# A second buffer for one output tile, and Q, residual and two additions in other places of a hand-written order

## The chip, the cores and the metric

The kernel runs on one core of one Trainium2 chip. The time is the device time of one execution in microseconds (us); the median of several runs is given. TensorE (PE) multiplies matrices, VectorE (DVE), ScalarE (ACT) and GpSimd (POOL) work on tiles, and SyncE (SP) issues the transfers. Each engine works through its own queue in order and waits on semaphores for the others.

## The reference

One layer of an encoder: 4096 tokens, width 1024, an attention group of 8 heads (2 key/value heads, band of 128 tokens on each side) and a pooling group, each gated, then an output projection, a norm and the residual.

```python
h = rmsnorm(x, pre_norm_g[l])
proj = jnp.einsum('bsd,de->bse', h, w_in[l])
q, k, v, g_a, u_p, g_p = jnp.split(proj, splits, axis=-1)
...
a = banded_attention(q, k, v, rel_bias, attn_sink[l]) * jax.nn.silu(g_a)
p = multiscale_pool(u_p, pool_w[l], pool_scale[l]) * jax.nn.silu(g_p)
mixed = jnp.einsum('bse,ed->bsd', jnp.concatenate([a, p], axis=-1), w_out[l])
x = x + rmsnorm(mixed, post_norm_g[l])
```

Inside `banded_attention`, each block of 128 queries sees three blocks of keys: scores, plus a position bias, then a softmax with a sink logit, then the weighted sum of V.

## The kernel before

A float32 value is carried as two float16 numbers, a high part and the low part that it leaves; a product of two such pairs is three float16 matmuls. The first half of the program (to about 500 us) computes the pooling group and the gates. The second half, which the change edits, runs backwards over 16 units of 256 tokens (two query blocks each; `u` is the unit, `b` the block, `half` a group of four heads). It is one list, `plan`: every step is entered with a due time by `due(t, step, ...)`, the list is sorted by that time, and the sorted order is the order on every engine. So a due time is not a time that a step waits for; it only says which steps stand ahead of it in each queue. The main loop runs from block 31 down to block 2; for the last units the due times are written out one by one (`at_`).

One visit of a block and half: TensorE makes `scores` (L1272); VectorE adds the bias and takes the maximum (`logits`, L1295); ScalarE makes the exponentials (L1306); VectorE the denominators (L1313) and their reciprocals (L1316); ScalarE the float16 probabilities `pn` (L1328, `probs`); VectorE what these leave (L1336, `rests`); SP turns both by a DMA transpose into `pt` (L1345), which TensorE multiplies with V in `values` (L1422). `gate` (L1446) multiplies the result with the gate into `at`.

Q for the next unit comes in two halves: TensorE's `proj_q` (L1227) fills a PSUM bank, then `keep_q` calls `split`: ScalarE writes the high part (L1216) and VectorE the low part (L1217), and after that the bank is free for the next half.

The output projection of a unit is a Strassen-like scheme of seven products (`product`, L1572, twelve matmuls of 512 columns each). The pieces are summed in two tiles of 128x1024 float32, `mo0` and `mo1`, one for each block of the unit. `begin` opens the unit's tiles (`open_unit`) and copies the first product from bank 0 into the second half of `mo0` (L1590), after which the product `12` adds into that bank. `add` (L1611), `gain11` (L1600), `square` (L1595) and `gain` (L1606) finish the tiles; `mean` makes the norm's factor; `residual` (L1633) multiplies `mo` with the factor and adds the input `xr`; `store` (L1639) writes the result. The casts to float16 pairs for the products are L1474 on ScalarE and L1478 on POOL.

`residual` of a unit's `mo0` is due late, in the next unit's visit, so it stands in VectorE's queue beside that unit's softmax. `mo0` and `mo1` have one buffer each (`bufs=1`).

Of the kernel before, what the change touches and what calls it, by code (L numbers as in the profile page):

```python
# [8 lines left out]
F32 = mybir.dt.float32  # L9
# [8 lines left out]
P = 128  # L18
S = 4096
D = 1024  # L20
# [114 lines left out]
def hybrid_layer(ctx: ExitStack, tc, io, out):  # L135
# [74 lines left out]
    with ExitStack() as actx:  # L210
# [689 lines left out]
        for j in range(4):  # L900
            ld(9.5 + 0.1 * j, wut[:, j], io["w_uT"][j], 0.5, w=[f"wut{j}"])
            z = turn("sq")
            for half in range(2):
                t = U0 + 4 * j + 2 * half
# [284 lines left out]
    pb = ctx.enter_context(tc.tile_pool(name="pb", bufs=2, reuse_waits="tile"))  # L1189
# [53 lines left out]
    def due(t, fn, *args):  # L1243
        plan.append((t, len(plan), fn, args))
# [216 lines left out]
    def spare32(tile, i):  # L1461

        return spare16(tile, 2 * D * i, 2 * D).bitcast(F32)
# [64 lines left out]
    LO, HI = slice(0, 512), slice(512, D)  # L1528
# [50 lines left out]
    def open_unit(u):  # L1579
        if u > 1:  # L1580
            mo_t[u] = [
                pb.tile([P, D], F32, name=f"mo{u}_{i}", tag=f"mo{i}", bufs=1) for i in range(2)
            ]
        else:
            mo_t[u] = [spare32("x", 2 * u + i) for i in range(2)]
        ss_t[u] = pb.tile([P, 4], F32, name=f"ss{u}", tag="ss")

    def begin(u):
        open_unit(u)
        nc.scalar.copy(mo_t[u][0][:, HI], z_t[u, 0])  # L1590
# [61 lines left out]
    def pe(us, fn, *args):  # L1652

        due(now[0], fn, *args)
        now[0] += us
        return now[0]
# [14 lines left out]
        due(t + late + 0.5, keep_v, u)  # L1671

    def do_q(u, half, late=0.0, bank=1):
        due(pe(5.3, proj_q, u, half, bank) - half + late, keep_q, u, half)

    def attend(b, bank):
        t = pe(2.0, values, b, bank)
# [36 lines left out]
    def mix_p3(u):  # L1714
        t = pe(M, product, u, "s4", O22, 1, True)
        due(t, add, u, (0, HI), (0, HI), 1)
        due(t + 0.7, square, u, 0, 1)
        due(t + 1.4, gain, u, 0, HI)
        due(t + 4.0, mean, u, 0)
        due(t + 12.4, residual, u, 0, LO)  # L1720
        due(t + 13.1, residual, u, 0, HI)
        due(t + 13.8, store, u, 0, slice(0, D))

    def finish(u, i, t):

# [6 lines left out]
    u = NU - 1  # L1732
# [6 lines left out]

    due(now[0] + 1.0, lambda: nc.scalar.activation(dummy, mhalf, AF.Exp))  # L1740
    do_q(u, 0)
    now[0] += 1.0
    for b in reversed(range(2, NB)):
        u = b // 2
# [5 lines left out]
        visit(b, 0)  # L1750
        if b == NB - 1:
            do_q(u, 1, 2.8, 0)
            due(now[0] + 0.1, load_x, u - 2)
            now[0] += 2.5
# [14 lines left out]
        elif b % 2:  # L1769
            mix_p3(u + 2)  # L1770
            do_kv(u - 1)
            attend(b + 1, 0)
            visit(b, 1)
            mix_p4(u + 1)
            mix_p1(u + 1)
            mix_p6(u + 1)
            mix_p2(u + 1)
        else:
            do_q(u - 1, 0, 2.0 * (b == NB - 2))
            if b < NB - 2:  # L1780
                attend(b + 1, 0)
            visit(b, 1)
            do_q(u - 1, 1, 2.0 * (b == NB - 2), int(b < NB - 2))
            due(now[0] + 2.1, load_x, u - 3)
            if b == NB - 2:
                attend(b + 1, 1)
            elif b > 2:
                mix_p7(u + 1)
                mix_p5(u + 1)
# [15 lines left out]
    def at_(t, fn, *args):  # L1805
        due(z + t, fn, *args)
# [11 lines left out]
    def cast(th, tw, u, name, f, eng):  # L1818
        at_(th, high, u, name, f)
        at_(tw, low, u, name, f, eng)  # L1820
# [36 lines left out]
    soft(0, 0, 24.9, 25.6, 29.4, 29.5, 29.7, 31.7)  # L1857
    soft(0, 1, 31.6, 32.3, 36.5, 36.7, 36.8, 38.8)

    at_(4.8, add, 2, (1, HI), (0, HI), 0)  # L1860
    at_(5.5, add, 2, (1, LO), (1, HI), 2)
    at_(6.2, add, 2, (1, HI), (1, HI), 1)
    at_(7.0, square, 2, 1, 0)
# [19 lines left out]
    at_(19.1, gain11, 1)  # L1883
    at_(17.8, square, 1, 0, 0, 0)
    cast(23.5, 24.2, 1, "s1", a_s1, V)
    at_(23.45, add, 1, (0, HI), (0, HI), 1)
    cast(24.8, 25.0, 1, "s4", a12, G)
    at_(27.0, add, 1, (1, HI), (0, HI), 0)
    at_(27.7, add, 1, (1, LO), (1, HI), 2)
# [15 lines left out]
    at_(45.9, gate, 0)  # L1905
    cast(46.7, 47.3, 0, "21", a21, V)
    at_(30.0, open_unit, 0)
    for i, t in ((0, 48.5), (1, 53.7)):
        for c in range(2):
# [92 lines left out]
```

## Time and profile before

| | us |
|---|---|
| median of 3 runs | 1193.59 (1192.48 to 1194.16) |
| the profiled execution | 1192.04 |
| its span in the profile | 1190.3 |
| TensorE busy | 1154.4 (97%) |
| VectorE busy | 941.9 (79%) |
| ScalarE busy | 703.8 (59%) |
| POOL busy | 303.4 (25%) |

A row of the timeline gives the start, the duration, the engine, the line, the operation, the tile written and the tiles read, the shapes, how many equal instructions are drawn together, and in brackets how long the engine had been idle and what ended that. "SPq" is SyncE's queue. Matmuls overlap each other, and their ends are modelled.

### The profile page before, as it was taken

The page shows a single profiled execution, that of the slowest core. Times are in us where ns is not written, and L with a number is a line of the kernel's source. Part 1 is how long each engine was busy: PE and PEld are TensorE (multiplying, and loading weights), DVE is VectorE, ACT ScalarE, POOL GpSimd, SP SyncE. Part 2 cuts the span into 40 slices and gives each one's busy share as a digit, 9 for nine tenths or more (in the row PEclk, how much of TensorE's full clock was granted, in tenths as well). Part 3 has the DMA queues.
Part 4 walks back from the last instruction along what each step waited for, and adds up shares of the span by engine and source line. Part 5 has one row for each costly group of instructions (what it writes and reads, how often), then busy time and mean ns, then how long its engine had stood idle before and what let it go on. Part 6 is the DMA issues. An engine that isn't in the chain of part 4 may idle for free. (4 is left out here: it accounts for less than half of the span.)

```text
span 1190.3 us, 33985 instructions
## 1 busy us (share of the span) xinstructions
PE 1154.4 (97%) x14304; PEld 884.8 (74%) x14304; DVE 941.9 (79%) x1879; ACT 703.8 (59%) x1459; POOL 303.4 (25%) x309
## 2 busy tenths in 40 slices
PE   5999999999999999998999999999999999999997
PEld 4998888888988888876667667576666667757643
DVE  6889996867888973567877878877887787787796
ACT  5865555545755541265666576666667667666662
POOL 0002111101101110203334434433533443343231
PEclk9999999999999999999999999999999999999999
DMA  9544587577657573397966876787886678586694
GB/s 318 208 124 151 169 277 246 171 239 259 221 169 249 156 212 117 117 242 174 253 181 147 188 189 128 200 196 142 192 193 177 145 191 192 135 190 164 156 245 124
DMA packets 292441, 224.65 MB, mean 189 GB/s; under 512 B 210704, under 2 KB 251920, under 8 KB 287680
## 3 DMA queue, kind: packets, MB, share of 16 engines
q1 hardware_dynamic: 292288, 222.48, 69.7%
q8 instruction: 112, 1.84, 0.6%
q14 instruction: 41, 0.34, 0.1%
HBM read 113.37 MB, written 60.33 MB: 146 GB/s over the span
## 5 line engine op out<-in xcount | busy, mean ns | idle before, releaser
L634 PEld LDWEIGHTS <-wq 128*128 128x128 f16 x4104 | 401.3, 98 | 53.1 <-issue 2.8
L634 PE MATMUL y<-xt,wq 128*128 128x256 f16 x1512 | 204.1, 273 | 0.9 <-ACT cc L742 0.9
L1336 DVE SCALAR_TENSOR_TENSOR pn<-p,rd,pn 128x384 f16<-128x384 f32 (+1 forms) x256 | 155.6, 654 | 31.8 <-ACT pn L1328 31.8
L1227 PE MATMUL aq<-xb,xb 128*128 128x256 f16 x1024 | 174.8, 274 | 1.7 <-DVE q L1217 1.6
L1306 ACT ACTIVATE p<-p,nm 128x385 f32<-128x385 f32 (+1 forms) x256 | 152.8, 598 | 33.3 <-POOL p L1289 22.4
L1572 PE MATMUL ms<-wo,ys 128*128 128x512 f16 x720 | 163.1, 379 | 1.7 <-ACT pn L1328 0.9
L1295 DVE CUSTOM_DVE_ANT_0 p<-s,nt,nsink 128x384 f32<-128x384 f32 (+1 forms) x256 | 155.9, 666 | 1.3 <-PE s L1272 1.1
L1328 ACT ACTIVATE pn<-p,rd 128x384 f16<-128x384 f32 (+1 forms) x256 | 136.4, 598 | 13.4 <-ACT p L1306 8.5
L1227 PEld LDWEIGHTS <-xb 128*128 128x128 f16 x1280 | 125.7, 98 | 23.3 <-issue 6.6
L1227 PE MATMUL aq<-xb,xt 128*128 128x256 f16 x512 | 140.3, 274 | 0.0
L1572 PEld LDWEIGHTS <-ys 128*128 128x128 f16 x720 | 69.0, 98 | 83.9 <-issue 3.3
L304 POOL TENSOR_TENSOR yt<-yt,sg 128x512 f32<-128x512 f32 (+2 forms) x32 | 48.0, 1501 | 311.3 <-DVE yt L307 302.3
L1572 PE MATMUL m<-wo,y 128*128 128x512 f16 x540 | 121.7, 379 | 2.8 <-ACT mo L1590 1.7
L1572 PEld LDWEIGHTS <-y 128*128 128x128 f16 x540 | 51.4, 98 | 68.3 <-issue 8.2
L1606 POOL TENSOR_TENSOR mo<-mo,gpost 128x512 f32<-128x512 f32 x39 | 63.6, 1630 | 86.8 <-ACT jkb L1595 85.7
L634 PE MATMUL plain<-xb,wq 128*128 128x256 f16 x576 | 68.8, 275 | 3.2 <-ACT xb L446 1.8
L1227 PEld LDWEIGHTS <-xt 128*128 128x128 f16 x640 | 62.9, 98 | 10.1 <-issue 1.5
L634 PE MATMUL y<-xb,wq 128*128 128x256 f16 x504 | 68.8, 273 | 0.0
L634 PE MATMUL v<-xb,wq 128*128 128x256 f16 x504 | 68.6, 273 | 0.2 <-DVE cc L304 0.2
L1272 PE MATMUL s<-k_all,q 64*32 64x288 f16 (+7 forms) x3648 | 62.9, 266 | 5.9 <-ACT q L1216 3.6
L634 PE MATMUL v<-xt,wq 128*128 128x256 f16 x504 | 68.6, 273 | 0.0
L634 PE MATMUL x<-xb,wq 128*128 128x256 f16 x504 | 68.3, 273 | 0.0
(211 smaller groups left out, 1917.1 us busy)
## 6 DMA issues: line engine op xcount, KB each, us to landing
nt<-in_xT SPq DMA_DIRECT2D x28, 512.0 KB, 5.2
x_scr<-xb SPq DMA_DIRECT2D x14, 1024.0 KB, 7.1
xb<-x_scr SPq DMA_DIRECT2D x14, 1024.0 KB, 7.6
xr<-in_x SPq DMA_DIRECT2D x28, 512.0 KB, 4.6
out<-xr SPq DMA_DIRECT2D x28, 512.0 KB, 2.8
xn<-in_x SPq DMA_DIRECT2D x27, 512.0 KB, 4.3
ga_scr<-cc SPq DMA_DIRECT2D x64, 128.0 KB, 2.2
raw<-in_w_out SPq DMA_DIRECT2D x16, 512.0 KB, 6.3
```

Of the source, the lines that this page charges most:

```text
L304: eng.tensor_tensor(out=out, in0=in0, in1=in1, op=op)
L634: nc.tensor.matmul(b[:, s], wq[:, slot[q, op], wv, s, k, :], x[:, xv, k, :], start=(first and k + s + wv + xv == 0), stop=(last and k == H ...
L1227: nc.tensor.matmul(acc, w[:, j, k, :], x[:, kh, v, kt, :], start=(n == 0), stop=(n == 3 * KT - 1),)
L1272: nc.tensor.matmul(s_ps[qs, gg, c0:c1], q_t[u, half][a, qi, jj, tl + 32 * hq : tl + 32 * hq + 32], k_all[a, ki, kc + c0 - s0 : kc + c1 - s ...
L1295: nc.vector.tensor_tensor_reduce(out=p_t[b, half][:, hh, :nk], in0=s_t[jj][:, gg, :nk], in1=bias[:, h, lo : lo + nk], scale=negc[:, h : h ...
L1306: nc.scalar.activation(p[:, hh, : nk + 1], p[:, hh, : nk + 1], AF.Exp, bias=nm_t[b, half][:, hh : hh + 1], scale=-1.0, accum_out=den_t[b, ...
L1328: nc.scalar.activation(prob_view(b, half)[:, 0, i], p_t[b, half][:, i, :nk], AF.Copy, scale=rd_t[b, half][:, i : i + 1],)
L1336: nc.vector.scalar_tensor_tensor(out=pn4[:, 1, i], in0=p_t[b, half][:, i, :nk], scalar=rd_t[b, half][:, i : i + 1], in1=pn4[:, 0, i], op0= ...
L1572: nc.tensor.matmul(z_t[u, tag], y[:, k, yi, :], wo[o][:, wi, k, :], start=(n == 0 and acc is None), stop=(n == 3 * HK - 1), skip_group_che ...
L1606: eng.tensor_tensor(out=mo, in0=mo, in1=gpost[:, cs], op=ALU.mult)
```

## The change

Four edits. `mo0` gets two buffers (`2 - i` is 2 for `i` = 0). The first half of Q is kept 1.0 us earlier by due time (the second half is where it was). The residual of `mo0` is no longer two halves, one ahead of the denominators and one behind the reciprocal, but one piece behind the reciprocal. In the written-out end, two additions come 1.1 us sooner.

```diff
         if u > 1:
             mo_t[u] = [
-                pb.tile([P, D], F32, name=f"mo{u}_{i}", tag=f"mo{i}", bufs=1) for i in range(2)
+                pb.tile([P, D], F32, name=f"mo{u}_{i}", tag=f"mo{i}", bufs=2 - i) for i in range(2)
             ]
...
     def do_q(u, half, late=0.0, bank=1):
-        due(pe(5.3, proj_q, u, half, bank) - half + late, keep_q, u, half)
+        due(pe(5.3, proj_q, u, half, bank) - 1.0 + late, keep_q, u, half)
...
         due(t + 4.0, mean, u, 0)
-        due(t + 12.4, residual, u, 0, LO)
-        due(t + 13.1, residual, u, 0, HI)
-        due(t + 13.8, store, u, 0, slice(0, D))
+        due(t + 13.1, residual, u, 0, slice(0, D))
+        due(t + 14.5, store, u, 0, slice(0, D))
...
-    at_(4.8, add, 2, (1, HI), (0, HI), 0)
+    at_(3.7, add, 2, (1, HI), (0, HI), 0)
...
-    at_(23.45, add, 1, (0, HI), (0, HI), 1)
+    at_(22.3, add, 1, (0, HI), (0, HI), 1)
```

VectorE, in the visit in which unit 7's tiles are opened, before (xr and mo are unit 8's residual, p, den, rd and pn the softmax of one half; the semaphores that a row waits for are in brackets):

```order
L1295 ISA nm_1_13733 128x1
L1633 SCALAR_TENSOR_TENSOR xr_13284<-mo_0_12969,rs_0_13573,xr_13284 128x512 [waits DMAHW5_49,DMAHW3_49,Pool_49]
L1313 TENSOR_SCALAR den_1_13734<-den_1_13734 128x4 [waits Activation_49]
L1316 RECIPROCAL rd_1_13735<-den_1_13734 128x4 [waits DVE_49]
L1633 SCALAR_TENSOR_TENSOR xr_13284<-mo_0_12969,rs_0_13573,xr_13284 128x512
L1336 SCALAR_TENSOR_TENSOR pn_1_13769<-p_1_13736,rd_1_13735,pn_1_13769 128x384 [waits DMAHW6_49,DVE_49,Activation_49]
```

The same place after:

```order
L1295 ISA nm_1_13726 128x1
L1313 TENSOR_SCALAR den_1_13727<-den_1_13727 128x4 [waits Activation_49]
L1316 RECIPROCAL rd_1_13728<-den_1_13727 128x4 [waits DVE_49]
L1633 SCALAR_TENSOR_TENSOR xr_13277<-mo_0_12962,rs_0_13566,xr_13277 128x1024 [waits DMAHW5_49,DMAHW3_49,Pool_49]
L1336 SCALAR_TENSOR_TENSOR pn_1_13761<-p_1_13729,rd_1_13728,pn_1_13761 128x384 [waits DMAHW6_49,Activation_49]
```

The two halves of the residual are one instruction behind the reciprocal, and the first rest follows it.

ScalarE at that place, before:

```order
L1306 ACTIVATE p_1_13736,den_1_13734<-p_1_13736,nm_1_13733 128x385 [waits DVE_49] x3
L1590 COPY mo_0_13763<-m_7_13748 128x512 [waits DVE_49,PE_49]
L1328 ACTIVATE pn_1_13769<-p_1_13736,rd_1_13735 128x384 [waits DMAHW6_49,Activation_49]
L1328 ACTIVATE pn_1_13769<-p_1_13736,rd_1_13735 128x384 [waits Activation_49]
L1328 ACTIVATE pn_1_13769<-p_1_13736,rd_1_13735 128x384
```

And after:

```order
L1306 ACTIVATE p_1_13729,den_1_13727<-p_1_13729,nm_1_13726 128x385 [waits DVE_49] x3
L1590 COPY mo_0_13755<-m_7_13741 128x512 [waits PE_49]
L1328 ACTIVATE pn_1_13761<-p_1_13729,rd_1_13728 128x384 [waits DMAHW6_49,DVE_49,Activation_49]
L1328 ACTIVATE pn_1_13761<-p_1_13729,rd_1_13728 128x384 [waits Activation_49]
L1328 ACTIVATE pn_1_13761<-p_1_13729,rd_1_13728 128x384
```

The order is the same, but the copy no longer waits for VectorE; the first probability does now.

ScalarE in the next stage, where the first half of the next unit's Q is kept, before:

```order
L1306 ACTIVATE p_0_13923,den_0_13921<-p_0_13923,nm_0_13920 128x385 [waits DVE_49] x3
L1328 ACTIVATE pn_0_13937<-p_0_13923,rd_0_13922 128x384 [waits DMAHW0_49,DVE_49,Activation_49]
L1328 ACTIVATE pn_0_13937<-p_0_13923,rd_0_13922 128x384 [waits Activation_49]
L1216 ACTIVATE q_0_13941<-aq_0_13870 128x512 [waits PE_49]
L1328 ACTIVATE pn_0_13937<-p_0_13923,rd_0_13922 128x384
```

And after:

```order
L1306 ACTIVATE p_0_13915,den_0_13913<-p_0_13915,nm_0_13912 128x385 [waits DVE_49] x3
L1216 ACTIVATE q_0_13929<-aq_0_13862 128x512 [waits PE_49]
L1328 ACTIVATE pn_0_13932<-p_0_13915,rd_0_13914 128x384 [waits DMAHW0_49,DVE_49,Activation_49]
L1328 ACTIVATE pn_0_13932<-p_0_13915,rd_0_13914 128x384 [waits Activation_49]
L1328 ACTIVATE pn_0_13932<-p_0_13915,rd_0_13914 128x384
```

Q's high part moves from between the probabilities to ahead of all four; on VectorE its low part moves from behind the first rest to ahead of it. In the written-out end, the first addition stands ahead of the fourth logits instead of behind it, and the second ahead of the last two rests instead of behind them.

## Prediction

> **What bounds the kernel now.** I read a table by stage first, then who TensorE waits for, then one period of the attention loop row by row. The execution of the loop is in lockstep, so one period speaks for the others. Columns of the stage table: the stretch, its length, and busy time with instruction counts for PE, PEld, DVE, ACT and POOL, then clock, DMA share and GB/s.
>
> ```profile
> 569.00:1126.00 557.00, 552.12 (x8276) 377.55 (x8283) 450.93 (x1028) 359.54 (x895) 216.13 (x223) 1.00 0.76 175
> 1126.00:1173.00 47.00, 45.51 (x540) 22.73 (x540) 41.99 (x95) 29.39 (x78) 13.98 (x14) 1.00 0.86 218
> ```
>
> From 569 to 1126 us, the loop that the change edits, TensorE is busy for 552.1 of 557 us. Nothing there can be worth more than TensorE's waits. Who it waits for in that stretch (total us, times, longest):
>
> ```profile
> PE m L1572 <- ACT mo L1590: 1.7, 9, 0.2
> PE aq L1227 <- DVE q L1217: 1.6, 7, 0.6
> ...
> PE o L1422 <- DMA pt<-pn: 0.2, 1, 0.2
> ```
>
> The first two are the copy of a product out of PSUM (`begin`, L1590) and the split of Q (`split`, L1217). These totals are too small. Here are TensorE's rows around both waits in the period of unit 7, and the longest Q wait:
>
> ```profile
> 889.04 5.35 PE L1572 MATMUL m<-wo,y 128*128 128x512 f16 x24
> 894.23 2.75 PE L1572 MATMUL ms<-wo,ys 128*128 128x512 f16 x12
> 897.17 2.75 PE L1572 MATMUL m<-wo,y 128*128 128x512 f16 x12 [0.19 <-ACT mo L1590]
> 899.85 0.93 PE L1272 MATMUL s<-k_all,q 64*32 64x288 f16 x48
> 900.71 0.28 PE L1227 MATMUL aq<-xb,xb 128*128 128x256 f16 x1
> ...
> 905.85 0.27 PE L1227 MATMUL aq<-xb,xb 128*128 128x256 f16 x1
> ...
> 907.97 0.93 PE L1272 MATMUL s<-k_all,q 64*32 64x288 f16 x48
> 909.09 0.27 PE L1227 MATMUL aq<-xb,xb 128*128 128x256 f16 x1 [0.18 <-DVE q L1217]
> ```
>
> From 889.04 to 894.23 are 24 products, so twelve take 2.595 us from start to start. The twelve from 894.23 need 2.94: the wait costs 0.345, not 0.19, because a matmul's drawn end covers part of the gap. In the same way scores to projection take 0.86 us unhindered (899.85 to 900.71) and 1.12 here: 0.26, not 0.18. The Trainium skill, Perfetto Trace Analysis, section Identifying the Most-Contended Engine, says that matmul busy share misjudges the room left because pipelined matmuls look smaller than they are. The trace agrees (0.19 drawn, 0.345 lost); by the drawn waits alone the two would be worth 3.3 us, and the starts decide.
>
> **Part 1: second buffer and later residual.** ScalarE and VectorE in that period:
>
> ```profile
> 894.86 0.18 ACT L1306 ACTIVATION_READ_ACCUMULATOR p<-p,nm 128x1 f32 x1
> 896.53 0.59 ACT L1590 COPY mo<-m 128x512 f32<-128x512 f32 x1 [1.49 <-DVE xr L1633]
> 897.01 2.13 ACT L1328 ACTIVATE pn<-p,rd 128x384 f16<-128x384 f32 x4
> 899.05 0.61 ACT L1474 CAST ys<-at 128x512 f16<-128x512 f32 x1
> 894.15 1.36 DVE L1633 SCALAR_TENSOR_TENSOR xr<-mo,rs,xr 128x512 f32<-128x512 f32 x1
> 895.43 0.16 DVE L1313 TENSOR_SCALAR den<-den 128x4 f32<-128x4 f32 x1
> 895.63 0.18 DVE L1316 RECIPROCAL rd<-den 128x4 f32<-128x4 f32 x1
> 895.72 0.72 DVE L1633 SCALAR_TENSOR_TENSOR xr<-mo,rs,xr 128x512 f32<-128x512 f32 x1
> 897.66 2.21 DVE L1336 SCALAR_TENSOR_TENSOR pn<-p,rd,pn 128x384 f16<-128x384 f32 x4 [1.22 <-ACT pn L1328]
> 893.69 1.27 POOL L1516 TENSOR_TENSOR yf<-yf,at 128x512 f32<-128x512 f32 x1
> 899.73 1.17 POOL L1478 TENSOR_TENSOR ys<-at,ys 128x512 f16<-128x512 f32 x1 [4.77 <-ACT ys L1474]
> ```
>
> ScalarE is free at 895.04, when its last exponential is read out, and the product to be copied is done (the next one begins at 894.23). The copy stands until 896.53 behind the second half of the residual of unit 8, which reads the same buffer, and the product after it on TensorE adds into the bank that it copies from. With two buffers it runs from about 895.04 to 895.63; TensorE wants the bank at 894.23 + 2.595 = 896.82, so there are 1.2 us to spare. Nine drawn waits at 0.345 give 3.1 us. The loop has 13 such copies waiting on the residual; the four undrawn ones cost between nothing and 0.17 each (what a drawn end can hide), and I take 0.12: 0.5. **3.6 us**, from 3.1 to 3.8.
>
> What is late next: denominators start at that same 895.04 instead of 895.43, the reciprocal ends near 895.46, and the probabilities start right behind the copy, near 895.6 instead of 897.01. The residual in one piece starts after the reciprocal, past the POOL operation that ended at 894.96 and had stretched the first half from 0.72 to 1.36; at 1.28 (its usual length in one piece, row below) it ends near 896.65. The four rests (what float16 leaves of the probabilities, L1336, 2.21 together) then start near 896.6 instead of 897.66 and end near 898.8 instead of 899.87. The store stands on SP's queue ahead of the transpose as before and issues some 0.2 us later; the transpose behind it waits for the rests anyway. TensorE's, POOL's and SP's own orders stay as they were. The second buffer moves other tiles in memory, so that the first weight loads of the loop wait for other transfers than before; I cost that at nothing, since none of TensorE's waits in the table is one for a weight.
>
> **Part 2: Q before the probabilities.** In the next stage:
>
> ```profile
> 905.52 0.60 ACT L1306 ACTIVATE p<-p,nm 128x385 f32<-128x385 f32 x1
> 906.71 1.12 ACT L1328 ACTIVATE pn<-p,rd 128x384 f16<-128x384 f32 x2 [0.50 <-ACT p L1306]
> 907.74 0.57 ACT L1216 ACTIVATE q<-aq 128x512 f16<-128x512 f32 x1
> 907.36 0.62 DVE L1336 SCALAR_TENSOR_TENSOR pn<-p,rd,pn 128x384 f16<-128x384 f32 x1 [0.73 <-ACT pn L1328]
> 908.34 0.69 DVE L1217 SCALAR_TENSOR_TENSOR q<-aq,q 128x512 f16<-128x512 f32 x1 [0.37 <-ACT q L1216]
> 568.01 0.93 PE L1272 MATMUL s<-k_all,q 64*32 64x288 f16 x48
> 569.50 0.27 PE L1227 MATMUL aq<-xb,xb 128*128 128x256 f16 x1 [0.56 <-DVE q L1217]
> ```
>
> TensorE's second projection needs the bank of the first, which the low part of Q (L1217) frees at 909.03. The high part (0.57) now goes into the 0.50 us in which ScalarE waits for the reciprocal, the low part (0.69) into the 0.73 in which VectorE waits for the first probability. Q is then done near 907.2, against a wish of 907.97 + 0.86 = 908.83. Worth 1.49 - 0.86 = 0.63 once and 0.26 in six others: **2.2 us**, from 1.5 (if a quarter of a microsecond stays in half of them) to 2.2. The new wait: four probabilities stand behind a copy that needs the first projection. That ends at 905.85 + 0.27 = 906.12, just as the exponentials end, so it costs them at most some tenths, and the rests still end earlier.
>
> **Part 3: the transposed probabilities.**
>
> ```profile
> DMA to landing us min/median/max: 5.1/6.5/10.5
> 899.95 3.66 SPq L1345 DMA_TRANSPOSE pt<-pn  x1
> 906.75 0.22 PE L1422 MATMUL o<-pt,vv 128*64 128x128 f16 x2
> ```
>
> The transpose of half 1 is issued at 899.95 and read at 906.75: 6.8 us for transfers with a median of 6.5. Part 1 issues it about 1.1 us sooner and its reader 0.35 sooner. The drawn 0.2 us wait should go: **0.3 us** (0.345 to 0.19, as above), from 0 to 0.9 (a few hidden ones).
>
> **Part 4: the two additions in the last units.**
>
> ```profile
> 1132.52 2.75 PE L1572 MATMUL m<-wo,y 128*128 128x512 f16 x12 [0.38 <-DVE mo L1611]
> 1152.78 2.94 PE L1572 MATMUL ms<-wo,ys 128*128 128x512 f16 x12 [0.79 <-DVE xb L1611]
> 1152.65 0.68 DVE L1478 TENSOR_TENSOR ys<-s,ys 128x512 f16<-128x512 f32 x1
> ```
>
> Both TensorE waits shrink, but here VectorE is the busy one (42.0 of 47 us), and its sum stays. The second product also needs the low part `ys` (to 1153.33), which stays where it was, so it gains nothing. The first addition (0.68) moves ahead of the last logits and pushes these, and ScalarE's last exponential behind them, back by some 0.6; the reciprocal that follows waits for that exponential and for two more additions, which hide most of it. **0.2 us lost**, from 0.6 lost (nothing hidden) to 0.4 gained (the whole first wait). The second addition moves ahead of two rests and delays their transpose by 0.68, whose reader (`values` of that block) has other products ahead of it; nothing.
>
> **Sum.** 3.6 + 2.2 + 0.3 - 0.2 = 5.9 us. The profiled execution took 1192.0 (span 1190.3), so 1186.1 there; the median of the runs is 1193.6, hence **1187.7**. Low ends together 4.0, high ends 7.3: 1186.3 to 1189.6 for this case.
>
> **Rivals.** *VectorE's last rest meets POOL.* The cast `ys` (899.05) moves up with the probabilities to about 897.6, and POOL's operation on it from 899.73 to about 898.24; the last rest would start near 898.15. If POOL comes first, the rest waits out its 1.17 us. That it can, these show:
>
> ```profile
> 924.79 1.28 DVE L1633 SCALAR_TENSOR_TENSOR xr<-mo,rs,xr 128x1024 f32<-128x1024 f32 x1 [0.36 <-POOL rs L1629]
> 925.99 2.69 DVE L1336 SCALAR_TENSOR_TENSOR pn<-p,rd,pn 128x384 f16<-128x384 f32 x3
> 924.84 2.37 POOL L1606 TENSOR_TENSOR mo<-mo,gpost 128x512 f32<-128x512 f32 x1
> ```
>
> Three rests need 2.69 us there, where four need 2.21 undisturbed. Then rests end near 900.0, the transpose leaves no sooner, its reader comes 0.35 sooner, and most of part 1 returns as a wait for the transpose: 2.5 us left, 1191.1. The Trainium skill, SBUF — State Buffer, section Who interferes with whom, has it as a rule: a VectorE operation with two SBUF inputs and a GpSimd one that reads SBUF lock each other out, whoever starts first. The trace agrees (2.69 and 2.37). By the starts the rest wins by 0.1 us, so chance 0.13.
>
> *No change.* The ScalarE-VectorE loop, not TensorE, sets the period, and TensorE's waits only come back elsewhere: 1193.6. For it: VectorE's 81% in the loop. Against: the same edits shorten that loop by the 1.49 us that ScalarE waits. 0.10.
>
> *Slower.* The Q copy holds ScalarE up: if the projection ended late, gate, logits and the next Q would be late, and its bank with them. To outweigh 5.9 and lose 2.4 more in 14 periods, the copy must wait over 0.6 us net in each, that is some 1.6 with the idle 0.50 and 0.73 used up; today projection and exponentials end together. Say 1197. 0.05.
>
> **Chances.** Forecast 0.72, POOL 0.13, no change 0.10, slower 0.05. A measurement tells about 0.2% (2.4 us) from no change, so faster takes 0.72 and over half of POOL: 0.80; same 0.15; slower 0.05. The range 1185.8 to 1191.4 leaves out the last two cases and a little at the low end, where the forecast's high end meets the spread of single runs.
>
> **What would show it.** Right: no TensorE wait for L1590 or L1217 in the loop; the copy right behind the exponentials; each period shorter by 0.35 us, and by 0.6 where Q waited. Wrong: rests longer than 0.62 beside L1478 on POOL, TensorE waits on `pt`, or a VectorE chain in the last units longer than before.

## The result, and the profile after

| | before | after |
|---|---|---|
| median of 4 runs (range), us | 1193.37 (1192.48 to 1194.16) | 1182.09 (1181.45 to 1182.63) |
| the profiled execution; its span, us | 1192.04; 1190.3 | 1182.25; 1180.4 |

The ratio is 0.9905 (95% interval 0.9888 to 0.9923): 11.3 us faster, where 5.9 were forecast; 1182.1 lies below the range. The spans differ by 9.9 us.

The stage table after, in the columns of the prediction's, and the only wait of TensorE that is drawn from 565 to 1126 us:

```profile
569.00:1126.00 557.00, 556.37 (x8339) 379.21 (x8337) 446.53 (x1030) 365.72 (x912) 223.06 (x225) 1.00 0.74 178
1126.00:1173.00 47.00, 45.72 (x508) 22.70 (x507) 40.12 (x85) 24.31 (x66) 12.79 (x14) 1.00 0.75 182
```

```profile
PE s L1272 <- issue: 0.6, 1, 0.6
```

TensorE is busy for 556.4 of 557 us, and its waits for L1590, L1217 and the transposed probabilities are gone. Here is the period of unit 7 again, which now lies 6.3 to 6.7 us earlier:

```profile
887.93 2.75 PE L1572 MATMUL ms<-wo,ys 128*128 128x512 f16 x12
890.52 2.75 PE L1572 MATMUL m<-wo,y 128*128 128x512 f16 x12
...
888.65 0.56 ACT L1590 COPY mo<-m 128x512 f32<-128x512 f32 x1
889.25 2.13 ACT L1328 ACTIVATE pn<-p,rd 128x384 f16<-128x384 f32 x4
...
889.10 1.28 DVE L1633 SCALAR_TENSOR_TENSOR xr<-mo,rs,xr 128x1024 f32<-128x1024 f32 x1
890.30 2.20 DVE L1336 SCALAR_TENSOR_TENSOR pn<-p,rd,pn 128x384 f16<-128x384 f32 x4
...
891.97 1.55 POOL L1478 TENSOR_TENSOR ys<-at,ys 128x512 f16<-128x512 f32 x1 [3.29 <-ACT ys L1474]
```

The product behind the copied one starts 2.59 us after the one before it (887.93 to 890.52; before, 2.94). The copy stands right behind the exponentials, the probabilities right behind the copy, the residual is one piece of 1.28, and the rests take 2.20.

So the waits that were forecast to go went, and the larger part of what was missing lies ahead of the loop. Where the first unit's attention begins (the hand-over), the two profiles read as follows, before first: ScalarE's first split of K and of Q, TensorE's first scores, and two slices of the stage table, whose third number from the end is the granted clock.

```profile
502.26 0.38 ACT L1216 ACTIVATE k_all<-kv 128x256 f16<-128x256 f32 x1 [4.77 <-DMA ga_scr<-cc]
...
504.94 0.58 ACT L1216 ACTIVATE q<-aq 128x512 f16<-128x512 f32 x1
...
505.57 0.30 PE L1272 MATMUL s<-k_all,q 64*32 64x256 f16 x8 [2.88 <-ACT q L1216]
...
506.00:508.00 2.00, 1.70 (x46) 1.26 (x47) 1.46 (x6) 0.57 (x3) 0.00 (x0) 0.80 0.98 414
508.00:510.00 2.00, 2.00 (x12) 1.41 (x10) 1.08 (x6) 1.51 (x7) 0.00 (x0) 0.50 1.03 438
```

```profile
498.05 0.38 ACT L1216 ACTIVATE k_all<-kv 128x256 f16<-128x256 f32 x1
...
503.24 0.60 ACT L1216 ACTIVATE q<-aq 128x512 f16<-128x512 f32 x1 [2.42 <-PE aq L1227]
...
503.89 0.30 PE L1272 MATMUL s<-k_all,q 64*32 64x256 f16 x8 [0.69 <-ACT q L1216]
...
506.00:508.00 2.00, 2.00 (x21) 1.80 (x19) 1.19 (x7) 1.83 (x8) 0.00 (x0) 1.00 0.96 406
508.00:510.00 2.00, 2.00 (x21) 1.78 (x20) 1.33 (x5) 1.67 (x4) 0.00 (x0) 1.00 1.06 446
```

Before, the split of K waited until 502.26 for stores (`ga_scr`) of the stage that ends there; Q's split stood behind it, TensorE stood idle for 2.88 us, and soon after that ran at a granted clock of 0.50. After, the split runs at 498.05, 4.2 us earlier, and the clock stays at 1.00. The program says why: the second buffer makes the pool that holds `mo0` 4 KB per partition larger, so that `k_all` lies 4096 bytes further on: over `cc3`, `cc4` and a few small tiles of the stage before instead of `cc1`, `cc2` and `cc3`. The split has to wait for fewer of the stores that read these tiles, and on the two queues that are left for earlier ones. ScalarE's row of that split before and after, with the queues that it waits for in brackets:

```
L1216 ACTIVATE k_all<-kv_5967 128x256 [waits DMAHW4_49,DMAHW5_49,DMAHW3_49,DMAHW6_49,PE_49,Activation_49]
L1216 ACTIVATE k_all<-kv_5967 128x256 [waits DMAHW5_49,DMAHW6_49,PE_49,Activation_49]
```

I laid TensorE's instructions of the two traces side by side, in the same order, and took the difference of their starts. Its steps say where the time went:

| place | step, us |
|---|---|
| up to 500 us (in the other profiles -0.1 to +1.1 against that of before) | +0.52 |
| hand-over: the wait before the first scores | -2.20 |
| hand-over: half clock behind it | -1.66 |
| hand-over: products and `values` up to 543 us | +1.23 |
| loop: 12 waits for the copy L1590 | -3.73 |
| loop: 8 waits for Q | -2.23 |
| loop: 4 waits for transposed probabilities | -1.20 |
| loop: the rest (the wait drawn as "issue" alone -0.39) | -0.22 |
| last units: at the first addition; at the second | -0.55; +0.20 |
| sum (spans: -9.9) | -9.84 |

### The profile page after: what moved, and what is told of

The parts are those of the page before. It is cut to its first block, busy times and chain, and to the rows that moved or that the text cites. A ratio compares the mean times of both kernels' runs of the same rounds, so it can differ in the third digit from the quotient of the medians.

```text
span 1180.4 us, 33944 instructions
## 1 busy us (share of the span) xinstructions
PE 1150.4 (97%) x14304; PEld 883.2 (75%) x14304; DVE 932.5 (79%) x1866; ACT 703.4 (60%) x1459; POOL 308.5 (26%) x309
## 4 chain that ended last, share of the span: by engine, by line
PE 49%; DVE 2%; ACT 1%; issue 1%; DMA 0%; DVEq 0%; POOLq 0%; ACTq 0%; SPq 0%
PE aq L1227 13%; PE ms L1572 12%; PE m L1572 9%; PE s L1272 4%; PE kv L1373 3%; PE o L1422 3%; PE kv L1227 3%; PE p L1422 2%; PE z L1544 1%; DVE pn L1336 1%; DVE p L1295 0%; DMA pt<-pn 0%; ACT pn L1328 0%; PE s L1544 0%; DVE mo L1611 0%
```

## Experiments

Two theories of the missing time were to be told apart, place in memory or chance, and the parts to be priced one by one. Later comparisons have medians of 1192.3 to 1192.5 us for the kernel before.

**The shift in memory alone (pad_only).**

```diff
+    pb.tile([P, D], F32, name="pad", tag="pad", bufs=1)
     q_t, v_t = {}, {}
```

> The kernel before with one unused tile of 128x1024 float32 more in the pool that holds mo0, so that everything behind it lies 4 KB further on in each partition, as in the changed kernel; no order is changed. Theory (place): before, the first split of K waits until 502.26 for the stores ga_scr that still read the memory under it, Q stands behind it, TensorE stands idle about 3 us and then runs at a granted clock of 0.5 for some 4 us; shifted, the split starts near 498 and the hand-over is some 2.6 us shorter: 1190.8 us or a little less. Rival (chance): the late split is a matter of when those stores happen to land in one execution, and no change of time is seen: 1193.4 us, the split again behind 501.

Measured: 1188.52 us (1188.21 to 1189.55) against 1192.42, ratio 0.997 (0.996 to 0.998): 3.9 us from an unused tile.

```profile
497.87 0.38 ACT L1217 ACTIVATE k_all<-kv 128x256 f16<-128x256 f32 x1
```

(The pad is a line more, so line numbers behind it are one higher in this kernel, and in the next one too.) The split of K runs at once, as in the changed kernel. The place theory holds; the rival falls. The gain is as large as the wait and the half clock together (2.20 + 1.66 = 3.86), and by the starts of TensorE both went. That the medians meet this sum is in part chance: in its profiled execution 0.44 came back at 541 us and 0.3 in the last units, and the span is 2.8 us shorter than that of the kernel before. The 2.6 expected had set the 1.23 of the table's next row against the two; 0.9 of that is put down to Q below.

**The changed kernel in the old place (after_oldplace).** The second buffer of `mo0` goes to a pool behind the others.

```diff
+    pbx = ctx.enter_context(tc.tile_pool(name="pbx", bufs=1, reuse_waits="tile"))
-                pb.tile([P, D], F32, name=f"mo{u}_{i}", tag=f"mo{i}", bufs=2 - i) for i in range(2)
+                (pbx if i == 0 and u % 2 else pb).tile(
+                    [P, D], F32, name=f"mo{u}_{i}", tag=f"mo{i}", bufs=1) for i in range(2)
```

> The changed kernel with the second buffer of mo0 in a pool of its own behind the others, so that the memory below it lies as in the kernel before; the orders stay as in the changed kernel. Theory (place): the first split of K waits for the stores again until about 502, and the time is 1182.1 plus about 2.6: 1184.7 us (up to 1186). The loop itself is as fast as in the changed kernel. Rival (chance): 1182.1 us.

Measured: 1186.75 us (1185.26 to 1188.54), ratio 0.9956 (0.9944 to 0.9969), 4.7 above the changed kernel. By the starts of TensorE it is 4.8 behind the changed kernel at 541 us, and from there to the end that difference hardly moves (5.2 at the end).

```profile
503.11 0.39 ACT L1217 ACTIVATE k_all<-kv 128x256 f16<-128x256 f32 x1 [5.02 <-DMA ga_scr<-cc]
...
506.42 0.41 PE L1273 MATMUL s<-k_all,q 64*32 64x256 f16 x8 [3.14 <-ACT q L1217]
...
508.00:510.00 2.00, 2.00 (x24) 1.16 (x9) 1.79 (x8) 1.51 (x7) 0.00 (x0) 0.50 1.02 430
510.00:512.00 2.00, 2.00 (x12) 1.37 (x10) 0.73 (x3) 1.49 (x6) 0.00 (x0) 0.50 1.03 434
```

The wait for the stores is back with all the orders of the changed kernel, 0.85 later than in the profile of before, and the slow clock lasts longer. In the program `k_all` lies where the kernel before has it, and in pad_only where the changed kernel has it. With the pad this shows the cause from both sides: 3.9 to 4.7 us are the place.

**The clock behind the wait (fill).** TensorE is given 2.6 us of work into the gap.

```diff
-        for jj in range(2):
+        for jj in (0, 1, 1) if (u, half) == (NU - 1, 0) else (0, 1):
             project_t(kv_t[u, half][:, jj], B_Q + 2 * half + jj, x_half(u))
```

> The kernel before with the second half of the first unit's Q projection (24 matmuls, 2.6 us) computed twice into the same bank; the result is the same. K's split still waits for the stores. TensorE then stands idle some 0.85 us instead of 3.05 ahead of the scores, which start about 0.3 later than before. Theory (clock): the granted clock stays at 1.0 behind them, and the 1.7 us (up to 3) that the projection lost at half clock are saved: 1191 us, in spite of 2.6 us of work more. Rival (the low clock is not set off by the idle time, but by something else at that place): 1192.7 us, the clock at 0.5 again.

```profile
503.17 0.38 ACT L1216 ACTIVATE k_all<-kv 128x256 f16<-128x256 f32 x1 [4.62 <-DMA ga_scr<-cc]
...
507.05 0.30 PE L1272 MATMUL s<-k_all,q 64*32 64x256 f16 x8 [0.69 <-ACT q L1216]
...
508.00:510.00 2.00, 2.00 (x55) 1.62 (x36) 1.74 (x7) 1.09 (x5) 0.00 (x0) 1.00 1.00 422
```

The split of K is as late as ever, TensorE's gap is 0.69 instead of 2.88, and the clock stays at 1.00: it is the idle time that brings the clock down here. By the starts of TensorE the scores come 0.42 later and the 1.67 of the half clock are saved, as expected; the time is 1191.80 us (1190.79 to 1192.43), ratio 0.9994 (0.9985 to 1.0002), which a gain of 1 us and none both fit. The Trainium skill, TensorE: Matmul & The Clock Gate, section Why this matters for your kernels, warns of idle gaps of more than about 3 us between bursts of matmuls. The trace agrees: drawn gaps of 2.88 and 3.14 lowered the clock, gaps of 0.69 didn't.

**The second buffer alone (buf_only, again as buf_b).**

```diff
-                pb.tile([P, D], F32, name=f"mo{u}_{i}", tag=f"mo{i}", bufs=1) for i in range(2)
+                pb.tile([P, D], F32, name=f"mo{u}_{i}", tag=f"mo{i}", bufs=2 - i) for i in range(2)
```

> The kernel before with the second buffer of mo0 alone. Theory: it carries both the shift in memory (2.6) and nearly all of the copy's gain (3.6 to 3.7, since the copy waits for nothing of VectorE's any more, wherever the residual stands): about 1187 us. Rival (residual needed): with the residual still ahead of the denominators, the probabilities stay late and half of the gain comes back as waits for the transpose: about 1189 us. Without the place theory it would be 1189.7 us.

Measured: 1182.28 us (1181.77 to 1182.71), ratio 0.9918 (0.9904 to 0.9931). All three figures expected were 4.7 us and more too high: the place counts 3.9, not 2.6, and the waits for Q and for the transposes went with the copy's. The buffer alone is as fast as the whole change. Six of TensorE's seven drawn waits for Q went too, though no Q was moved. At unit 7, on POOL, TensorE and VectorE, of buf_only:

```profile
895.57 0.32 POOL L1289 COPY p<-nsink 128x4 f32<-128x4 f32 x2
...
893.23 0.28 PE L1227 MATMUL aq<-xb,xb 128*128 128x256 f16 x1
...
901.36 0.28 PE L1227 MATMUL aq<-xb,xb 128*128 128x256 f16 x1
...
900.45 0.69 DVE L1217 SCALAR_TENSOR_TENSOR q<-aq,q 128x512 f16<-128x512 f32 x1 [0.37 <-ACT q L1216]
```

Before, on POOL:

```profile
903.48 0.32 POOL L1289 COPY p<-nsink 128x4 f32<-128x4 f32 x2
```

Counted from the start of the first projection (900.71 before, 893.23 here), POOL's copy, which the exponentials of this half wait for, comes at 2.34 instead of 2.77: the softmax and the casts ahead of it got free of the copy's wait. Q's low part ends at 7.91 instead of 8.32, and TensorE wants the bank at 8.13. A wait in one stage had made the one in the next.

**Q alone (q_only).**

```diff
-        due(pe(5.3, proj_q, u, half, bank) - half + late, keep_q, u, half)
+        due(pe(5.3, proj_q, u, half, bank) - 1.0 + late, keep_q, u, half)
```

> The kernel before with Q's first half kept 1.0 us earlier by due time, and nothing else. Theory: TensorE's waits for the split of Q go, 2.2 us: 1191.2 us. Rival (the copy's wait grows in their place, or the wait moves to the transposes): 1192.5 to 1193.4 us.

Measured: 1191.53 us (1190.67 to 1193.01), ratio 0.9995 (0.9986 to 1.0004): no gain that can be told. By the starts of TensorE all the waits for Q went (0.63, and 0.25 six times), but 0.93 was lost at 543 us, much as in the changed kernel, and 1.2 at the hand-over, where the clock stayed at 0.50 for 6.8 us instead of 3.4:

```profile
508.00:510.00 2.00, 2.00 (x38) 1.22 (x23) 1.71 (x7) 1.07 (x5) 0.00 (x0) 0.50 1.06 446
510.00:512.00 2.00, 2.00 (x12) 1.41 (x10) 0.58 (x4) 1.49 (x7) 0.00 (x0) 0.50 0.96 406
512.00:514.00 2.00, 2.00 (x14) 1.56 (x13) 1.68 (x4) 1.23 (x4) 0.13 (x1) 0.68 1.02 426
```

Whether the move of Q has a part in that longer stretch, one trace can't say.

**All but Q (after_no_q).**

> The changed kernel with Q's first half kept when it was before. Theory (the buffer does Q's work too): in the kernel with the buffer alone, six of the seven waits of TensorE for the split of Q had gone without any move of Q; only the one of 0.63 near 569 stays, and the move costs 1.23 at 541 us, where Q's low part stands ahead of two rests. So 1182.1 + 0.63 - 1.23 = 1181.5 us, no wait for L1217 in the loop but one. Rival (the prediction's part 2): the waits of Q come back, 2.2 us: 1184.3 us.

Measured: 1181.73 us (1181.56 to 1183.16), ratio 0.9913 (0.99 to 0.9927). One wait for Q is left:

```profile
PE aq L1227 <- DVE q L1217: 0.6, 1, 0.6
```

The prediction's 2.2 us for Q were real as waits, but with the buffer there the move of Q is worth 0.63 and costs 0.9 (TensorE's step at 541 us between this kernel and the changed one).

**The residual alone (res_only).**

```diff
-        due(t + 12.4, residual, u, 0, LO)
-        due(t + 13.1, residual, u, 0, HI)
-        due(t + 13.8, store, u, 0, slice(0, D))
+        due(t + 13.1, residual, u, 0, slice(0, D))
+        due(t + 14.5, store, u, 0, slice(0, D))
```

> The kernel before with the residual in one piece behind the reciprocal, and one buffer. The product's copy then waits for the whole residual (1.28 us) behind the reciprocal, until about 896.65 instead of 896.53 in the period of unit 7. Theory (the buffer is the part that counts): no gain, 0 to 0.15 us lost in each of 13 periods: 1192.5 to 1194.5 us. Rival (the later residual is itself a gain, since denominators start earlier and probabilities with them): 1190 us.

Measured: 1195.73 us (1194.61 to 1197.57), ratio 1.0028 (1.0016 to 1.0039): 3.4 slower. TensorE's waits for the copy:

```profile
PE m L1572 <- ACT mo L1590: 4.7, 12, 0.4
```

They are 4.7 us drawn instead of 1.7, a step of 0.23 in most periods by the starts. Without the second buffer the later residual is a loss, larger than expected; with it, buf_only and the changed kernel have the same loop, and it is worth nothing.

**A better version (best, again as best_b).** Q moves only from the third unit on, and the second addition goes back.

```diff
-    do_q(u, 0)
+    do_q(u, 0, 1.0)
-            do_q(u - 1, 0, 2.0 * (b == NB - 2))
+            do_q(u - 1, 0, 3.0 * (b == NB - 2))
-    at_(22.3, add, 1, (0, HI), (0, HI), 1)
+    at_(23.45, add, 1, (0, HI), (0, HI), 1)
```

> The changed kernel with Q moved earlier only in the loop (where the first two units' first halves of Q are kept, the order of before), and with the second of the two additions in the last units back in its place. Theory: 1.23 less at 541 us, 0.2 less at 1146 us: 1182.1 - 1.4 = 1180.7 us. Rival (the wait at 541 us is for the transposes' queue and comes back behind it): 1182 us.

Measured: 1181.00 us (1180.86 to 1181.82), ratio 0.9907 (0.9891 to 0.9922). ScalarE and VectorE in the second unit's first visit, and the product that waits in the end, of the changed kernel:

```profile
524.00 2.13 ACT L1328 ACTIVATE pn<-p,rd 128x384 f16<-128x384 f32 x4 [0.80 <-DMA pt<-pn]
524.65 1.15 DVE L1336 SCALAR_TENSOR_TENSOR pn<-p,rd,pn 128x384 f16<-128x384 f32 x2 [1.03 <-ACT pn L1328]
526.65 0.69 DVE L1217 SCALAR_TENSOR_TENSOR q<-aq,q 128x512 f16<-128x512 f32 x1 [0.85 <-ACT q L1216]
527.26 1.14 DVE L1336 SCALAR_TENSOR_TENSOR pn<-p,rd,pn 128x384 f16<-128x384 f32 x2
...
537.88 0.60 PE L1572 MATMUL m<-wo,y 128*128 128x512 f16 x2 [0.93 <-ACT y L1474]
```

And of the better version:

```profile
523.64 2.13 ACT L1328 ACTIVATE pn<-p,rd 128x384 f16<-128x384 f32 x4 [0.50 <-DVE rd L1316]
524.28 2.20 DVE L1336 SCALAR_TENSOR_TENSOR pn<-p,rd,pn 128x384 f16<-128x384 f32 x4 [0.73 <-ACT pn L1328]
526.41 0.68 DVE L1217 SCALAR_TENSOR_TENSOR q<-aq,q 128x512 f16<-128x512 f32 x1
```

In the changed kernel Q's low part stands ahead of two rests here, while on ScalarE the high part still stands behind all four probabilities. VectorE idles 0.85 for it, with two rests behind it; they end at 528.4 instead of 526.5. The next softmax and the casts behind it are late by as much, a product waits for one of them, and `values` starts 1.23 later (541.56 against 540.27, less 0.07 by which the traces differ already). With Q back in its place, that is gone. Not all of it is Q's: the probabilities start 0.3 late too, because they wait for a transpose to land (0.80 of idle time instead of 0.50). That wait is in some executions without any move of Q (0.3 us in after_no_q, 0.44 in pad_only) and not in others, which leaves 0.9 for Q. The 0.2 expected of the second addition did not come: TensorE is 1.28 earlier than in the changed kernel both before that place and behind it.

To settle so small a difference, the three ran side by side on one chip:

> The changed kernel once more, beside the next two on the same chip. By its other runs: 1182.1 us.

> The better version once more (Q earlier only in the loop, the second addition in its old place). Theory: the step of 1.23 us at 541 us is real and nothing takes its place: 1.1 us under the changed kernel beside it. Rival: the difference of 1181.0 and 1182.1 us was that of two sessions, and both are the same.

> The second buffer alone once more. Theory (the other three edits together are worth 0.3 to 0.5 us, from -0.63 at 569, +1.23 at 541, -0.54 and +0.2 in the last units): within 0.6 us of the changed kernel. Rival (they are worth the 2.2 us of the prediction's part 2): 2 us above it.

| | median (range), us | ratio to before |
|---|---|---|
| after_b | 1182.71 (1181.74 to 1183.03) | 0.9921 (0.9906 to 0.9936) |
| best_b | 1181.19 (1180.66 to 1181.38) | 0.9909 (0.9894 to 0.9924) |
| buf_b | 1181.90 (1181.10 to 1182.64) | 0.9913 (0.9897 to 0.993) |

In both comparisons (the first one across two sessions) the better version lies 1.1 to 1.5 us under the changed kernel, and here their ranges don't meet; both are far under the kernel before. The ratios' intervals, which carry the spread of the kernel before, overlap. The second buffer alone is level with the whole change.

## Why the prediction was wrong

**The step that failed** is the sentence in part 1 on the second buffer that moves other tiles: "I cost that at nothing, since none of TensorE's waits in the table is one for a weight." It looked at weights, and at a table that began at 569 us; the tile that mattered was `k_all`, and the wait for it lay at 505 us, ahead of the table, where 2.88 us of idle TensorE and a clock of 0.50 stood in the profile. Measured alone, it is 3.9 us (pad_only) to 4.7 (after_oldplace).

**Part 1, the copy:** 3.6 forecast, 3.73 measured; right in place and size (twelve waits: nine of about 0.35 and three of 0.16 to 0.19, where thirteen with four of 0.12 were taken). One reading needs a correction: a product's matmuls are drawn longer than they take (0.379, where one starts 0.216 after another), not smaller, so their drawn busy time hides room; the sum, taken from the starts, is untouched. But the later residual has no share in it: the buffer alone does it, and the residual alone costs 3.4.

**Part 2, Q:** 2.2 forecast, 2.23 of waits gone. Right as a sum; wrong as to its cause, since the buffer alone removes all but 0.63. The new wait that I priced at "some tenths" came, on VectorE instead of ScalarE, and once: 0.9 of the 1.23 at 541 us, much as in my slower rival, in one place.

**Part 3, transposes:** 0.3 forecast, 1.20 measured, over the bound of 0.9. Only one of the four waits stood in the table; the other three were wholly or mostly hidden in drawn ends.

**Part 4, two additions:** 0.2 lost forecast, 0.35 gained measured. The first wait went whole (0.55), which was my outer bound; VectorE, the busy engine there, was early by only some 0.35, so TensorE waits out 0.20 of it again at the second product. The second addition has no share in that: with it back in its old place (best) the 0.20 stays.

**The rivals.** POOL and VectorE did meet: POOL's L1478 took 1.55 instead of 1.16 or 1.17. But it was POOL that waited; the rests kept their 2.20. No change and slower are out.

By the trace the sum is 9.8, with 3.9 for the place, and 1.2 lost at 541 us ahead of the loop. That 5.9 forecast and 3.9 for the place make this sum too is luck: those 1.2 and the 0.5 up to 500 us, on one side, met 1.3 more than forecast in the loop and 0.55 in the last units. The rest of the 11.3 goes with a spread: the kernel before ran from 1190.5 to 1194.4 in the later comparisons, and kernels in the old place split K between 502.26 and 503.55 in their profiles. The spread goes along with the clock, though not with it alone: of its 41 later executions, the five with a mean granted clock of 0.999 took 1190.5 to 1191.9 us, the twelve with 0.995 or 0.996 took 1193.1 to 1194.4. That this alone makes the difference is likely, not shown; the changed kernel beside it later was 9.8 us faster by the medians (1192.47 and 1182.71).

## What to carry to other kernels

A buffer more is also a move of everything that lies behind it: list which instructions wait for other queues than before, and look each of them up in the trace over the whole span, above all where one stage hands its memory to the next. When waits of two neighbouring stages are priced, try first whether the one makes the other; parts that add up as waits need not add up as edits. And look in each place, the first and the last rounds too, whether a moved instruction still follows its producer on the other engine.

## Not expected of the hardware

The idle gap of TensorE at the hand-over cost more than itself. Behind a drawn gap of 2.88 us (before) or 2.99 (res_only) the granted clock was 0.50 for 3.4 us, behind one of 3.04 (q_only) or 3.14 (after_oldplace) for 6.8 us; by the starts of TensorE that is 1.7 us lost in the kernel before and 2.6 in after_oldplace. In after_oldplace the low clock began before the matmuls did (505.8 against 506.42), in the kernel before some 2 us after them (from 507.6 on, one projection matmul is drawn with 0.42 where 0.27 is usual). Whether the length of the gap decides between 3.4 and 6.8 us, four traces can't show.
